# The last merge of a hybrid layer: low halves made by adding DMAs instead of GpSimd and VectorE subtractions

## The chip, the cores and the metric

The kernel runs on one core of a Trainium2 chip. The metric is the device time of one execution in microseconds. The engines are TensorE (PE, with its weight loads as PEld), VectorE (DVE), ScalarE (ACT), GpSimd (POOL) and SyncE (SP), which here only issues DMAs. Each engine works through its own queue in order. A DMA is issued by SP, or by POOL where it has to add to what stands at its destination; the data are then moved by 16 DMA engines that all queues share.

## The reference

One layer with two token groups, 128 context tokens and 512 latent tokens (640 in all), model width 1024:

```python
h = _rmsnorm(x, p["norm1_g"]) * (1.0 + sc1) + sh1
u_rw, u_na, gate_rw, gate_na = jnp.split(h @ p["w_in"], IN_SPLITS, axis=-1)
o_rw, s_new = _rwkv_branch(u_rw, s0, ...)
...
merged = (jax.nn.sigmoid(gate_rw) * (o_rw @ p["w_o_rwkv"])
          + jax.nn.sigmoid(gate_na) * (o_na @ p["w_o_na"]))
x = x + g1 * (merged @ p["w_out"])
h2 = _rmsnorm(x, p["norm2_g"]) * (1.0 + sc2) + sh2
x = x + g2 * ((jax.nn.silu(h2 @ p["ffn_w1"]) * (h2 @ p["ffn_w3"])) @ p["ffn_w2"])
```

o_rw and o_na have 512 features each, that is four blocks of 128. The change lies where `merged` is completed and multiplied by w_out.

## The kernel before, in words

All products are float32, computed in three passes: each operand is split into a high half (a cast to the fp32r type) and a low half (the value minus the cast high half), and TensorE adds high by high, high by low and low by high. So every weight tile of 128x1024 and every activation needs a cast (ScalarE, line 173 for weights, 185 and 1580 for activations) and a low half. For a weight tile `wcast` (166) makes the low half in one of two ways. With `eng` left out, VectorE subtracts (175). With `eng` = pool, ScalarE first writes the negated tile, rounded to fp32r, into the low tile (171), and POOL then issues a DMA that adds the staged weights to it (172). 37 weight tiles take this second way in the kernel before. For an activation `split` (184) casts and subtracts on a given engine (186).

The kernel runs through the projections, neighbourhood attention and the recurrent branch, the merge, w_out and the feed-forward part. The merge goes over eight output blocks of 128 features (index c8). Units "a" and "b" of `merge_gen` (1453) have already added up the products of seven of the eight feature blocks of o into `mt[c8]`. The eighth, the last output of the recurrent branch, is written by `out` (1388) for ct = 3 into two tiles `o3`, one high and one low, in two halves of 320 tokens; PRM["yo"] names for each ct the engine that makes the low half (1419).

Then comes the last merge, `last_gen` (1566). `wo` (1564) is the weight tile for the eighth feature block; `c0` (1589) is the first tile of w_out. For each c8 and each half (a, b) of 320 tokens, a group, `last_gen` issues three matmuls of wo by o3 (1576) into a PSUM tile, of which there are three, multiplies by the gate on VectorE (1577), adds `mt` on VectorE (1579), casts to the high half `mh` on ScalarE (1580) and makes the low half `ml` on POOL (1581). Tiles mh and ml hold the merged activation m; in the profile both are called m, and the gate tiles t are called pre (c8 under 4) and tr (the others).

`w_out_gen` (1585) multiplies m by w_out; it goes through `tok_gen` (261) with line 284. It takes the four weight tiles of the first half of the output columns in turn; with each it goes over two blocks of m, for the four latent token tiles and then the context tile, and for each of these three matmuls: mh by the weight's high half, ml by the high half, mh by the low half. The loop at 1593 weaves the two: PRM["lw"] is 0 for the first five groups and 2 for the other eleven, so after group 5 (counted from 0) and after each later one two matmuls of w_out are issued; the rest follows at the end (1597). 

In this block only TensorE's order is the written one (MANUAL, 78). Where VectorE, ScalarE, POOL and SP take up each instruction is set by a planner that simulates the program while it is built. In the recurrent part before and the second half of w_out behind it, TensorE, POOL, VectorE and ScalarE have a written order (FIRST, 79).

Weight tiles are staged by SP loads into `wst` buffers, two in the pool that wo and c0 use; the next tile that takes such a buffer can only be loaded when its last reader is done, be it an engine or a DMA. In the same stretch SP loads the five tiles of x (1548), the gate rows G (1553), the tiles t of the last four blocks (1570) and further tiles of w_out.

Of the kernel before, what the change touches and what calls it, by code (L numbers as in the profile page):

```python
# [7 lines left out]
F32 = mybir.dt.float32  # L8
F32R = mybir.dt.float32r
AF = mybir.ActivationFunctionType  # L10
ALU = mybir.AluOpType
# [58 lines left out]
    fp=(6, 12, 18), h2e="dpddddpddd", x0e="a", ze="aa", y2=1, y1=0, sc=3, sr=3, sp=1, mg=1.915, h1=0.952,  # L70
    h2=0.91, jobs=((2, 9, 28), (2, 9, 28), (2, 9, 28), (2, 11, 28)),
    mds=((4, 12), (4, 12), (4, 12), (4, 14)), bud=((1.8, 0.8), (1.3, 1.8)), off=6, tk=2, h3=1,
    h4=1.07, g1=2, km="dddddddd", kb="ddpd", ma="d", yo="pppp", r0="pd", rl=(0, 0, 0), lh=(0, 0, 1, 1),
    wl="dddddddddppppppppppppppppppppppppppdpppppppppppp", nu=9, jo=(2, 0, 1), na=(
        "6.0.12.0.1 6.0.12.0.0 6.0.12.0.0 6.0.12.0.2 6.0.12.0.0 6.0.12.0.2 6.0.12.0.0 6.0.12.0.2 6.0.12.0.0 "
        "6.0.12.0.2 6.0.12.1.0 6.1.12.1.2 6.2.12.2.0 6.1.12.2.2 6.0.12.2.0 6.1.12.1.2 6.2.14.2.0 "
# [25 lines left out]
def V(ap, dims, off=0):  # L102

    return bass.AP(ap.tensor, ap.offset + off, [list(ap.ap[0])] + [list(d) for d in dims])
# [3 lines left out]
def body(ctx: ExitStack, tc: tile.TileContext, xs, xp, cols, consts, w_ada, b_row, w_rw, w_qkv,  # L108
# [3 lines left out]
    pe, act, dve, pool, sp = nc.tensor, nc.scalar, nc.vector, nc.gpsimd, nc.sync  # L112

    def open_pool(stack, name, bufs=1, space=None):
        if space is None:
            return stack.enter_context(tc.tile_pool(name=name, bufs=bufs, reuse_waits="tile"))
        return stack.enter_context(tc.tile_pool(name=name, bufs=bufs, reuse_waits="tile", space=space))
# [17 lines left out]
    def nm(s):  # L135
        cn[0] += 1
        return f"{s}_{cn[0]}"
# [19 lines left out]
    def wdma(src, home=None):  # L157
        if len(rot) > 1 and home is None:
            rot.append(rot.pop(0))
        pl, nst, nhl = (rot if home is None else wpool)[-1 if home is None else home] if rot else wpool[-1]  # L160
        st = pl.tile([P, 1024], F32, tag="wst", bufs=nst, name=nm("wst"))
        n = src.shape[1] if len(src.shape) == 2 else 1024
        sp.dma_start(st[:, :n] if len(src.shape) == 2 else V(st[:, :], [[128, 8], [1, 128]]), src)
        return st, n, pl, nhl

    def wcast(w, eng=None):
        st, n, pl, nhl = w
        hi = pl.tile([P, 1024], F32R, tag="whi", bufs=nhl, name=nm("whi"))
        lo = pl.tile([P, 1024], F32R, tag="wlo", bufs=nhl, name=nm("wlo"))
        if eng is pool:  # L170
            act.activation(lo[:, :n], st[:, :n], AF.Copy, scale=-1.0)  # L171
            pool.dma_start(lo[:, :n].bitcast(F32), st[:, :n], accum_op=ALU.add)  # L172
        act.copy(hi[:, :n], st[:, :n])  # L173
        if eng is not pool:
            dve.tensor_tensor(out=lo[:, :n], in0=st[:, :n], in1=hi[:, :n].bitcast(F32), op=ALU.subtract)  # L175
        return hi, lo

    def wload(src, eng=None):
        return wcast(wdma(src), eng)
# [135 lines left out]
    def hilo(n):  # L315
        return [hp.tile([P, 8, NT], F32R, tag=f"hp{i}", bufs=1, name=f"{n}{i}") for i in range(2)]
# [141 lines left out]
    def pre_t():  # L458
        return kp.tile([P, 643], F32, tag="pre", bufs=4, name=nm("pre"))[:, :NT]
# [320 lines left out]
    with s1:  # L780
# [25 lines left out]
        with s1a:  # L806
            for b, dst, gcol in ((0, qT, dcol(dqg)), (1, kT, col("kg"))):
# [10 lines left out]
                for i in range(5):  # L818
# [10 lines left out]
                                      in0=V(qr[:, :], [[64, 8], [1, 64]]),  # L829
                                      in1=V(r[:, :], [[1, 8], [0, 64]]), op=ALU.mult)  # L830
                    if b == 1 and i == 4:
                        kout = tb.tile([P, 512], F32, tag="vt", bufs=2, name="kout")
                        dve.tensor_tensor(out=V(kout[:, :], [[64, 8], [1, 64]]),
                                          in0=V(qn[:, :], [[64, 8], [1, 64]]),
                                          in1=V(kgb[:, :], [[0, 8], [1, 64]]), op=ALU.mult)
# [4 lines left out]
                    for f in range(4):  # L840
                        src = pst[:, f * 128:(f + 1) * 128]
                        if i < 4:
                            out = V(dst[f], [[1, 2], [8, 64]], 2 * i)
                            src = V(src, [[64, 2], [1, 64]])
                        else:
                            out = dst[f][:, 512:640]
# [27 lines left out]
        with ExitStack() as s1b:  # L874
# [127 lines left out]
            with tc.manual_schedule(engines=FIRST):  # L1002
                for k, step in enumerate(PRM["na"].split()):
                    a, p, b, q, n = (int(x) for x in step.split("."))
# [556 lines left out]
    pp = open_pool(ctx, "pp4", bufs=3, space=PSUM)  # L1561

    mh, ml = hilo("m")
    wo = wload(w_o[:, :, 896:1024].rearrange("c p n -> p c n"))

    def last_gen():
        ts_ = []
        for c8 in range(8):
            t = pre_t() if c8 < 4 else trp.tile([P, NT], F32, tag="tr", bufs=4, name=nm("tr"))
            sp.dma_start(t, trw_d[c8])  # L1570
            ts_.append(t)
        for c8, t in enumerate(ts_):
            for (a, b) in halves:
                ps = pp.tile([P, 512], F32, tag="tp", name=nm("fl"))
                for n, (w, x) in enumerate(((wo[0], o3[0]), (wo[0], o3[1]), (wo[1], o3[0]))):
                    pe.matmul(ps[:, :H2], w[:, c8 * 128:c8 * 128 + 128], x[:, a:b], start=n == 0, stop=n == 2)
                dve.scalar_tensor_tensor(out=t[:, a:b], in0=t[:, a:b], scalar=1.0, in1=ps[:, :H2],
                                         op0=ALU.add, op1=ALU.mult)
                dve.tensor_tensor(out=t[:, a:b], in0=mt[c8][:, a:b], in1=t[:, a:b], op=ALU.add)
                act.copy(mh[:, c8, a:b], t[:, a:b])  # L1580
                pool.tensor_tensor(out=ml[:, c8, a:b], in0=t[:, a:b], in1=mh[:, c8, a:b].bitcast(F32),
                                   op=ALU.subtract)
                yield

    def w_out_gen(pss, ws, toks, **kw):
        return tok_gen(pss, pp, (mh, ml), ws, list(range(8)), toks, **kw)

    pss = {}
    c0 = wload(w_out[0])
    trp = open_pool(hs, "trp")  # L1590
    weights(hs, 2, 2)
    w0 = w_out_gen(pss, [c0] + [w_out[q] for q in range(1, 4)], range(5))
    with tc.manual_schedule(engines=MANUAL):
        for h, _ in enumerate(last_gen()):
            for _ in range(PRM["lw"][h]):
                next(w0)
        drain(w0)
# [378 lines left out]
def _build(arrays):  # L1976
    import concourse.bacc as _bacc

    nc = _bacc.Bacc("TRN2", target_bir_lowering=False, num_devices=1)
    args = [nc.dram_tensor(f"in_{n}_dram", v.shape, mybir.dt.from_np(v.dtype), kind="ExternalInput").ap()  # L1980
            for n, v in arrays.items()]
    args += [nc.dram_tensor(f"out_{i}_dram", s, F32, kind="ExternalOutput").ap()
             for i, s in enumerate(_OUTS)]
    with tile.TileContext(nc, **TCARGS) as tc:
        body(tc, *args)
    return nc
# [12 lines left out]
```

## Time and profile before

| | |
|---|---|
| median of 3 runs (lowest to highest) | 1192.29 us (1192.16 to 1193.37) |
| profiled execution, its time and its span | 1191.72 us, 1189.7 us |
| mean granted TensorE clock | 0.985 |
| TensorE busy | 1124.1 us (94%) |
| VectorE, ScalarE, POOL busy | 777.5, 530.5, 205.1 us |
| the last merge (first to last matmul of line 1576) | 679.0 to 695.3 us |
| first half of w_out complete | 720.77 us |

The last merge stands in the middle of the span. Times inside the span are counted from its first instruction. The page gives the busy time of every engine, the chain of work that ended last, and groups of instructions; the timeline gives the instructions of one engine in order, with the idle time before them and what ended it in brackets; stretches of the span can be asked for by engine, with the granted clock of TensorE (1.00 is full) and the busy share of the 16 DMA engines.

### The profile page before, as it was taken

Reading aid. Unit: us, or ns where it says so; the run is one execution under the profiler, and the core shown is the slowest. Engines: PE = TensorE matmul, PEld = TensorE weight load, DVE = VectorE, ACT = ScalarE, POOL = GpSimd, SP = SyncE. Lnnn points to the kernel's source line nnn. Section 1 sums busy time; section 2 is a strip of 40 time slices with the busy share of each in tenths; the row PEclk is TensorE's granted clock in tenths of the full one; section 3 lists DMA queues with packets and bytes.
Section 4 is the critical chain, followed back from the end, with each engine's and each line's share of the span. In section 5 each row is a group of like instructions: output and inputs, shape, how many; then the busy total and the mean of one; then the engine's idle time right before and its main releaser. Section 6 shows DMA issues by size and latency. Waiting matters only on the chain.

```text
span 1189.7 us, 26921 instructions
## 1 busy us (share of the span) xinstructions
PE 1124.1 (94%) x11160; PEld 998.3 (84%) x11160; DVE 777.5 (65%) x1630; ACT 530.5 (45%) x1053; POOL 205.1 (17%) x273
## 2 busy tenths in 40 slices
PE   6999999999999999999599799989999999999998
PEld 4688877789888988888488678889899989998997
DVE  4564455559469658836474675888568757775675
ACT  4444666554564664565133342654224422442340
POOL 1162244320111211111101250100001000000000
PEclk9999999999999999999799999999999999999999
DMA  9762767553333514433654851312312231232122
GB/s 335 265 117 84 244 216 230 191 146 98 103 93 84 153 50 104 123 93 79 200 138 110 245 218 54 107 49 79 104 57 86 89 107 54 89 100 90 59 75 103
DMA packets 61906, 149.42 MB, mean 126 GB/s; under 512 B 7732, under 2 KB 23732, under 8 KB 61784
## 3 DMA queue, kind: packets, MB, share of 16 engines
q1 hardware_dynamic: 55592, 131.56, 33.6%
q0 software_dynamic: 5328, 14.94, 6.8%
q8 instruction: 88, 1.44, 0.5%
q10 hardware_dynamic: 864, 1.20, 0.3%
q14 instruction: 34, 0.28, 0.1%
HBM read 118.41 MB, written 14.32 MB: 112 GB/s over the span
## 4 chain that ended last, share of the span: by engine, by line
PE 65%; DVE 8%; ACT 3%; DMA 2%; issue 1%; SPq 0%; ACTq 0%; DVEq 0%; POOLq 0%
PE f L1718 23%; PE acc L284 17%; PE fl L197 13%; DMA wlo<-wst 1%; DVE pr L1250 1%; PE w L1324 1%; PE w L1351 1%; DVE RL L1254 1%; PE mm L197 1%; PE w L1364 1%; PE w L1336 1%; PE w L1148 1%; DMA o<-o_d 1%; PE w L1196 1%; PE w L1126 1%
## 5 line engine op out<-in xcount | busy, mean ns | idle before, releaser
L1718 PE MATMUL f<-t,whi 128*128 128x320 f32 x640 | 141.4, 309 | 0.0
L1718 PE MATMUL f<-b,whi 128*128 128x320 f32 x608 | 136.5, 312 | 3.6 <-ACT b L185 1.8
L284 PE MATMUL acc<-whi,u 128*128 128x512 f32 (+1 forms) x448 | 136.0, 385 | 0.0
L197 PE MATMUL fl<-h,whi 128*128 128x320 f32 x704 | 126.5, 319 | 0.8 <-issue 0.8
L197 PEld LDWEIGHTS fl<-h,whi 128*128 128x128 f32 x704 | 106.1, 188 | 5.6 <-issue 0.9
L173 ACT CAST whi<-wst 128x1024 fp32r<-128x1024 f32 (+2 forms) x86 | 81.5, 953 | 64.7 <-PE acc L284 32.5
L1718 PEld LDWEIGHTS f<-t,whi 128*128 128x128 f32 x640 | 107.1, 188 | 0.0
L1718 PEld LDWEIGHTS f<-b,whi 128*128 128x128 f32 x608 | 103.0, 190 | 4.8 <-ACT b L185 2.2
L1718 PE MATMUL f<-t,wlo 128*128 128x320 f32 x320 | 98.9, 309 | 0.0
L284 PEld LDWEIGHTS acc<-whi,u 128*128 128x128 f32 x448 | 83.5, 188 | 16.7
L1718 PE MATMUL f<-b,wlo 128*128 128x320 f32 x304 | 94.7, 312 | 1.4 <-DVE wlo L1762 1.4
L1759 ACT CAST whi<-ws 128x1024 fp32r<-128x1024 f32 x40 | 42.0, 1051 | 108.7 <-PE f L1718 48.5
L1773 POOL TENSOR_TENSOR ws<-wst 128x512 f32<-128x512 f32 x20 | 28.2, 1409 | 341.3 <-DVE wlo L1762 226.7
L175 DVE TENSOR_TENSOR wlo<-wst,whi 128x1024 fp32r<-128x1024 f32 (+1 forms) x49 | 62.0, 1274 | 37.2 <-ACT whi L173 36.6
L284 PE MATMUL acc<-wlo,u 128*128 128x512 f32 (+1 forms) x224 | 86.3, 385 | 0.0
L284 PE MATMUL acc<-whi,h 128*128 128x512 f32 x240 | 78.0, 399 | 1.2 <-DVE h L398 1.1
L172 POOL DMA_DIRECT2D wlo<-wst x37 | 32.6, 881 | 232.4 <-ACT wlo L171 212.9
L1558 DVE SCALAR_TENSOR_TENSOR tt<-acc,G 128x512 f32<-128x512 f32 (+1 forms) x51 | 34.7, 681 | 50.5 <-PE acc L284 50.5
L197 PE MATMUL fl<-h,wlo 128*128 128x320 f32 x352 | 66.5, 321 | 0.0
L197 PE MATMUL fl<-o,whi 128*128 128x320 f32 x224 | 46.3, 337 | 16.8 <-DMA o<-o_d 10.0
L1759 ACT CAST whi<-wst 128x1024 fp32r<-128x1024 f32 (+1 forms) x48 | 41.3, 869 | 42.3 <-PE acc L284 37.6
L1718 PEld LDWEIGHTS f<-t,wlo 128*128 128x128 f32 x320 | 60.1, 188 | 0.0
(333 smaller groups left out, 2539.1 us busy)
## 6 DMA issues: line engine op xcount, KB each, us to landing
wst<-in_w_dram SPq DMA_DIRECT2D x66, 512.0 KB
wst<-in_w_rw_dram SPq DMA_DIRECT2D x31, 512.0 KB
wa<-in_w_ada_dram SPq DMA_DIRECT2D x24, 512.0 KB
wlo<-wst POOLq DMA_DIRECT2D x22, 512.0 KB, 4.5
f<-in_w_ada_dram SPq DMA_DIRECT2D x16, 512.0 KB
wst<-in_w_qkv_dram SPq DMA_DIRECT2D x12, 512.0 KB
o<-o_d SPq DMA_DIRECT2D x14, 320.0 KB
x<-in_xs_dram SPq DMA_DIRECT2D x8, 512.0 KB
```

Of the source, the lines that this page charges most:

```text
L172: pool.dma_start(lo[:, :n].bitcast(F32), st[:, :n], accum_op=ALU.add)
L173: act.copy(hi[:, :n], st[:, :n])
L175: dve.tensor_tensor(out=lo[:, :n], in0=st[:, :n], in1=hi[:, :n].bitcast(F32), op=ALU.subtract)
L197: pe.matmul(ps[:, :t1 - t0], w[:, a:a + 128], x[:, k0 + kt, t0:t1], start=n == 0, stop=n == 3 * nk - 1)
L284: pe.matmul(pss[i][:, a:b], lhs(x, kt, ts_), w[:, cs_], start=ki == 0 and n == 0, stop=ki == last and n == 2)
L1126: pe.matmul(t[r0:r0 + 32, 64 * i:64 * i + 64], S.BK[l // 10][own, l % 10, 0, 32 * bk:32 * bk + 32], V(AG[own, l, h, :], [[0, 2], [1, 32]], ...
L1148: pe.matmul(pr[h][hrows[h ^ i], o_], x[hrows[h], :], R_[hrows[h], l, :], start=True, stop=True)
L1196: pe.matmul(pt[h][hrows[h ^ i], o_], S.BK[l // 10][hrows[h], l % 10, i, :], idh(h), start=True, stop=True)
L1558: dve.scalar_tensor_tensor(out=tt, in0=ps[:, a:b], scalar=c, in1=G[:, g, sl], op0=ALU.mult, op1=ALU.mult)
L1718: pe.matmul(ps[:, :H2], w_[:, c_], x_[:, kt, :], start=first and kt + n == 0, stop=last and kt == 3 and n == 2, skip_group_check=more)
L1759: act.copy(r[0][:, :width], src())
L1773: eng_x(PRM["se"][i - 1]).tensor_tensor(out=o_, in0=x, in1=y, op=op)
```

## The change

The low half of `wo` and of `c0` is made with `eng` = pool: a negation on ScalarE, and a DMA issued by POOL that adds the staged weights. For c8 from 0 to 5, `ml` is made in the same manner: ScalarE negates each half of t into ml, and after the second half one DMA, issued by POOL, adds the whole t (128 x 640, 320 KB) to it. For c8 of 6 and 7, VectorE subtracts. The low half of the last output `o3` is made by VectorE instead of POOL. POOL has no tensor operation left in the last merge.

```diff
-    h4=1.07, g1=2, km="dddddddd", kb="ddpd", ma="d", yo="pppp", r0="pd", rl=(0, 0, 0), lh=(0, 0, 1, 1),
+    h4=1.07, g1=2, km="dddddddd", kb="ddpd", ma="d", yo="pppd", r0="pd", rl=(0, 0, 0), lh=(0, 0, 1, 1),
...
-    wo = wload(w_o[:, :, 896:1024].rearrange("c p n -> p c n"))
+    wo = wload(w_o[:, :, 896:1024].rearrange("c p n -> p c n"), pool)
...
                 act.copy(mh[:, c8, a:b], t[:, a:b])
-                pool.tensor_tensor(out=ml[:, c8, a:b], in0=t[:, a:b], in1=mh[:, c8, a:b].bitcast(F32),
-                                   op=ALU.subtract)
+                if c8 < 6:
+                    act.activation(ml[:, c8, a:b], t[:, a:b], AF.Copy, scale=-1.0)
+                    if a:
+                        pool.dma_start(ml[:, c8, :].bitcast(F32), t, accum_op=ALU.add)
+                else:
+                    dve.tensor_tensor(out=ml[:, c8, a:b], in0=t[:, a:b], in1=mh[:, c8, a:b].bitcast(F32),
+                                      op=ALU.subtract)
                 yield
...
-    c0 = wload(w_out[0])
+    c0 = wload(w_out[0], pool)
```

## The prediction

> **What bounds the kernel now.** I read the busy shares and the chain that ended last, then the chain in order of time around the last merge, then the timelines of the engines there.
>
> ```profile
> PE 1124.1 (94%) x11160; PEld 998.3 (84%) x11160; DVE 777.5 (65%) x1630; ACT 530.5 (45%) x1053; POOL 205.1 (17%) x273
> ...
> PE 65%; DVE 8%; ACT 3%; DMA 2%; issue 1%; SPq 0%; ACTq 0%; DVEq 0%; POOLq 0%
> ```
>
> ```profile
> 648.52 0.28 issue
> ...
> 675.80 1.24 DVE wlo L175
> ...
> 677.05 0.33 SPq L163
> ...
> 700.53 20.24 PE acc L284 x88
> ```
>
> TensorE is the bound. From 700.53 us on it runs without a break: 88 matmuls in 20.24 us are 0.23 us each, and the first half of w_out is complete at 720.77. The stretch after that is just as full:
>
> ```profile
> 676.00:679.00 3.00, 0.00 (x0) 0.00 (x1) 2.97 (x5) 0.60 (x3) 1.53 (x1) 1.00 0.31 74
> 679.00:684.00 5.00, 4.45 (x16) 3.82 (x17) 4.97 (x11) 1.62 (x3) 1.23 (x2) 0.58 1.00 400
> 679.85:686.65 6.80, 6.28 (x21) 5.68 (x21) 6.80 (x12) 1.37 (x4) 3.08 (x4) 0.50 1.00 405
> 684.00:692.00 8.00, 7.43 (x35) 6.46 (x34) 8.00 (x14) 2.78 (x7) 7.08 (x8) 0.84 1.03 415
> 701.00:1186.00 485.00, 479.79 (x2808) 444.31 (x2806) 340.54 (x477) 171.02 (x250) 36.91 (x30) 1.00 0.25 83
> ```
>
> (Columns: length, then busy time of PE, PEld, DVE, ACT, POOL, granted clock, DMA share, GB/s.) TensorE is busy 479.79 of 485 us, so what the end of the first w_out half gains or loses against 720.77 goes to the end of the kernel one for one. The whole question is the stretch from 676 to 701, where TensorE does not run full, the granted clock is 0.50 for 6.8 us, and the DMA engines are full (1.00 to 1.03).
>
> ```profile
> 675.34 0.60 PE L197 MATMUL fl<-o,wlo 128*128 128x320 f32 x3
> 679.03 0.53 PE L1576 MATMUL fl<-o,whi 128*128 128x320 f32 x2 [3.09 <-ACT o L185]
> ...
> 683.04 0.73 PE L1576 MATMUL fl<-o,whi 128*128 128x320 f32 x2
> ...
> 683.85 0.73 PE L1576 MATMUL fl<-o,whi 128*128 128x320 f32 x2
> ...
> 684.64 1.05 PE L284 MATMUL acc<-whi,m 128*128 128x512 f32 x2
> ...
> 692.26 0.46 PE L1576 MATMUL fl<-o,whi 128*128 128x320 f32 x2
> ...
> 692.71 0.40 PE L284 MATMUL acc<-wlo,m 128*128 128x512 f32 x1
> ...
> 700.53 0.50 PE L284 MATMUL acc<-wlo,m 128*128 128x512 f32 x1 [2.02 <-DVE wlo L175]
> ```
>
> The order on TensorE is written by hand: six groups of three L1576 matmuls (high by high, low by high, high by the weight's low), then two w_out matmuls, a group, two, and so on. The two at 684.64 are the first users of m: the first reads the high half of block 0, the second, at about 684.64+0.43 = 685.07, its low half. A group costs 0.45 us at full clock (692.26 to 692.71) and 0.81 at half (683.04 to 683.85).
>
> **The change part by part.** In these rows are the operations it touches:
>
> ```profile
> 674.72 1.05 ACT L173 CAST whi<-wst 128x1024 fp32r<-128x1024 f32 x1 [4.01 <-PE fl L197]
> ...
> 678.52 0.46 ACT L185 CAST o<-out 128x320 fp32r<-128x320 f32 x1 [2.40 <-DVE out L1412]
> ...
> 683.31 0.82 ACT L1580 CAST m<-pre 128x320 fp32r<-128x320 f32 x2 [3.38 <-PE fl L1576]
> ```
>
> ```profile
> 680.41 1.21 DVE L175 TENSOR_TENSOR wlo<-wst,whi 128x1024 fp32r<-128x1024 f32 x1
> 681.55 1.27 DVE L1577 SCALAR_TENSOR_TENSOR pre<-pre,fl 128x320 f32<-128x320 f32 x3
> ```
>
> ```profile
> L1579 DVE TENSOR_TENSOR pre<-mt,pre x8: 477/804/1209, 682.7 to 689.6; 128x320 f32<-128x320 f32 x8
> ```
>
> ```profile
> 676.21 1.53 POOL L186 TENSOR_TENSOR o<-out,o 128x320 fp32r<-128x320 f32 x1 [6.58 <-ACT o L185]
> 679.06 1.08 POOL L186 TENSOR_TENSOR o<-out,o 128x320 fp32r<-128x320 f32 x1 [1.32 <-ACT o L185]
> 683.85 2.78 POOL L1581 TENSOR_TENSOR m<-pre,m 128x320 fp32r<-128x320 f32 x3 [3.71 <-ACT m L1580]
> ```
>
> The kernel already makes 37 low halves by an adding DMA (L172). Their landing times are the prices of the change:
>
> ```profile
> DMA to landing us min/median/max: 2.9/4.5/8.5
> ```
>
> ```profile
> wlo<-wst POOLq DMA_DIRECT2D x1, 192.0 KB, 5.8
> ...
> wlo<-wst POOLq DMA_DIRECT2D x1, 256.0 KB, 8.5
> ...
> wlo<-wst POOLq DMA_DIRECT2D x1, 512.0 KB, 6.4
> ...
> wlo<-wst POOLq DMA_DIRECT2D x1, 512.0 KB, 4.4
> ```
>
> ```profile
> 664.39:669.39 5.00, 4.02 (x27) 3.52 (x27) 2.66 (x6) 1.66 (x4) 3.52 (x3) 1.00 1.01 276
> 565.23:570.23 5.00, 0.00 (x0) 0.00 (x0) 0.00 (x0) 0.21 (x1) 0.92 (x1) 0.69 0.97 311
> 259.69:264.69 5.00, 3.72 (x172) 3.27 (x172) 1.56 (x2) 2.71 (x4) 2.46 (x4) 1.00 1.01 223
> 296.42:301.42 5.00, 5.00 (x123) 4.57 (x124) 4.81 (x9) 2.76 (x6) 0.85 (x1) 1.00 0.62 138
> ```
>
> The four landings belong to the four stretches in the same order: under full DMA engines 5.8 us for 192 KB, 8.5 for 256 KB, 6.4 for 512 KB; with room (0.62), 4.4 for 512 KB.
>
> **wo's low tile.** Removed: one VectorE subtraction of 1.24 us that ended at 677.04, long before its first use (679.40). Added: a ScalarE negation as long as the cast, 1.05 us (674.72 to 675.77), 0.28 us to the issue (the 648.52 row), a DMA issue on POOL at 676.05, and a landing. Bounds 4.4 and 6.4 us; the DMA share is 0.31 up to 679 and 1.00 after, so I take 5.0, nearer the quiet row: 681.05. The third matmul of the first group waits for it, and with it everything on TensorE. The SP load that waited for the same staging buffer (677.05) now waits for the landing too, with the loads of x and of four merge tiles queued behind it on SP, or it is moved behind those; none of them has a reader on TensorE's path before 691, so nothing is charged.
>
> **The last output's low half on VectorE.** POOL's 1.53 and 1.08 us go, two VectorE operations of some 0.48 (the shortest L1579) come. The output is complete near 678 instead of 680.14. Worth nothing: the first group's third matmul waits for wo until 681.05.
>
> **c0's low tile.** The subtraction at 680.41 (1.21 us), which stood right in front of the first L1577, goes; the DMA that replaces it is queued on POOL ahead of m's first one and needs wo's route again. Its tile is first read after m's low half, so nothing is charged; the VectorE time it frees counts in the next step.
>
> **m's low halves.** Before, POOL made each half-block in about 0.93 us (2.78 for three) behind its cast, and TensorE had no wait for it. Now block 0 needs both halves: two casts and two negations on ScalarE, an issue, a landing. From wo's landing: the third matmul 0.47 at half clock; from the first L1577 to the end of both casts 2.58 us (681.55 to 683.31+0.82); 0.8 more, since the three L1577 that run first now wait for groups 1 and 2 at 0.81 each instead of finding them done; 0.41 for the last negation (half of 0.82); 0.28 to the issue. That is 4.54, so the issue is at 685.59. For 320 KB no row exists. Between 2.9 (the shortest of all) and 8.5, in a stretch whose share is 1.03, I take 6.0, between the 5.8 and the 6.4 of the full rows: landing at 691.59, where before the matmul ran at 685.07. During that wait TensorE has only what is left of the first six groups (681.05 + 0.47 + 5 x 0.81 = 685.6), VectorE and ScalarE run dry behind it, and POOL and SP have nothing that helps.
>
> What TensorE still has to do then is 119 w_out matmuls and 10 groups: 119 x 0.23 + 10 x 0.45 = 31.9 us. Blocks 1 to 5 land while it works on block 0's 12 matmuls and after; charged nothing. The subtractions of blocks 6 and 7 (four of 0.48 on VectorE) are covered, because VectorE's L1579 are no longer stretched: 0.48 instead of 0.80 in the median. The 2.02 us wait for VectorE's wlo at 700.53 goes for the same reason; next late there is the same tile's own cast and load, which I charge nothing. ScalarE's 14 new operations (12 x 0.46 + 2 x 1.05 = 7.6 us) fit into its idle time (1.37 busy of 6.8).
>
> **The clock.** A stall of some 6 us comes right before 691.59. Here 3.09 idle us were followed by 6.8 us at 0.50, and elsewhere a busy TensorE stood at half clock for 3.4 us:
>
> ```profile
> 345.30:348.70 3.40, 3.40 (x30) 3.08 (x29) 2.38 (x4) 2.23 (x6) 0.00 (x0) 0.50 0.78 154
> ```
>
> Half clock costs half its length of full work: 1.7 to 3.4 us; I take the middle, 2.5.
>
> **Sum.** 691.6 + 31.9 + 2.5 = 726.0 against 720.77: +5.2 us. The profiled execution took 1191.72 (span 1189.7), 0.57 under the median, so I add to the median: 1192.29 + 5.2 = 1197.5. Bounds of the unknown costs: high, wo 6.4, m 8.5, clock 3.4: 676.05+6.4+4.54+8.5+31.9+3.4 = 730.8, +10.0, 1202.3; low, wo 4.4, a chain without the 0.47 and the 0.8 (3.27), m 2.9, clock nothing: 676.05+4.4+3.27+2.9+31.9 = 718.5, -2.3, 1190.0.
>
> **The rule weighed.** Row first: 512 KB never landed in this trace under 4.4 us. The Trainium skill (DMA: Bandwidth & Descriptors, "Anatomy of one DMA") fits a POOL-issued DMA as 2.0 us plus bytes over 436 GB/s, an estimate of 3.2 us for 512 KB and 2.75 for 320 KB. By it the sum would be 676.05+3.2+4.54+2.75+31.9+2.5 = 720.9, no change; the trace disagrees by 1.2 us at least.
>
> **The rivals.** Each as a mechanism with its price.
> - The DMA engines leave the adds alone: both land with no other traffic in the way. The full share (1.03) speaks against it; that SP may hold its loads back behind wo's staging buffer speaks for it. wo 4.4 and m about 3.7 (between the 2.9 and the 4.4): 676.05+4.4+4.54+3.7 = 688.7, a stall of 3.7 us (from 680.45+0.47+4.05 = 685.0); if the clock holds, 688.7+31.9 = 720.6: 1192.1. By the rule above much the same comes out.
> - Faster: the freed VectorE outruns the adds. Without the subtraction at 680.41 and with unstretched L1579 the first block is ready early, and m's add takes the trace's shortest time: the low bound, 1190.0 and under. It decides from a landing before 686.5 on (686.5+31.9 = 718.4, 0.2% gained). For it speak POOL's share in the stretches above; against it that TensorE has nothing to do before wo lands.
> - Worse: the adds meet the burst of loads as at 565.23, where 256 KB took 8.5 us. Then 695.5 and the high bound, 1202.3. For it: the same share and the same mix of HBM loads; against it: one such landing in 37.
> - The change does not do what it says, that is VectorE's relief and the adds both stay off the path (wo's low tile lands before the last output is ready, m's before its use): it needs wo in under 3.4 us, which no 512 KB row shows.
>
> **How the numbers follow.** Forecast (a stall, then half clock, 1195 to 1200) 0.50; the burst 0.16; the quiet DMAs with the clock held 0.15, and the page's fit 0.03, both without change; the faster case 0.14, of which 0.11 beyond the bound; no moved limit 0.02, without change. 0.2% (2.4 us) is about what a measurement of this kernel can tell from none. Slower 0.66, same 0.23, faster 0.11. The range reaches from the low bound to the high one, 1190.0 to 1202.3; the forecast's own is 1195 to 1200.
>
> **What would show it.** Right: TensorE waits at L1576 for a DMA of wlo near 681 and at the second L284 for a DMA of m for 4 to 7 us; a granted clock of 0.50 behind that; L1579 near 0.48; no 2.02 us at the next wlo; the first w_out half ends near 726. Wrong: m's add lands within 4 us of its issue, the planner finds an order that has wo's add issued earlier, the clock stays at 1.00, or TensorE's later stretch is not full and swallows the shift.

## The result and the profile after

| | before | after |
|---|---|---|
| median (lowest to highest) | 1192.43 us (1192.16 to 1193.37) | 1208.08 us (1205.78 to 1209.56) |
| ratio, 95% interval | | 1.0127 [1.0112, 1.0142] |
| profiled execution, its span | 1191.72, 1189.7 us | 1209.56, 1207.7 us |
| first half of w_out complete | 720.77 us | 738.92 us |

The change costs 15.6 us, three times the forecast of 5.2. The kernel after is the slower one on the whole interval, and above the forecast's range (1202.3).

The profiled execution of after is 1.5 us over its median, that of before 0.7 under. Of the difference between the two, 2.1 us are older than the first instruction that the change touches: an adding DMA that both kernels have, ahead of the last merge, starts 1.47 us later and takes 0.63 longer, and the load of wo waits for it (issued at 670.21 in before, at 672.30 in after). The chain of before, and then the chain of after:

```profile
664.39 5.76 DMA wlo<-wst
```

```profile
665.86 6.39 DMA wlo<-wst
```

This 2.1 us is called the shift below. So 18.15 us between the two ends of the first w_out half, less 2.1, are 16.1 us that the changed stretch adds in this execution. Behind it TensorE is as full as before (460.03 busy of 465.10 us), so what is lost here is lost for good. TensorE's timeline shows where:

```profile
680.15 1.66 PE L197 MATMUL fl<-o,whi 128*128 128x320 f32 x6 [1.84 <-DVE mx L1464]
682.59 0.87 PE L1576 MATMUL fl<-o,whi 128*128 128x320 f32 x2
683.26 0.47 PE L1576 MATMUL fl<-o,wlo 128*128 128x320 f32 x1
...
686.25 0.40 PE L284 MATMUL acc<-whi,m 128*128 128x512 f32 x1
697.44 0.77 PE L284 MATMUL acc<-whi,m 128*128 128x512 f32 x1 [10.79 <-DMA m<-pre]
...
709.34 0.90 PE L1576 MATMUL fl<-o,whi 128*128 128x320 f32 x2 [5.28 <-DVE tr L1577]
```

Three waits are to be read here: 1.84 us for VectorE ahead of the merge, 10.79 us for m's first add, and 5.28 us for VectorE in the middle of it. The third matmul of the first group, on wo's low tile (683.26), waits for nothing. The stretches between (length, then PE, PEld, DVE, ACT, POOL, granted clock, DMA share, GB/s) show what TensorE could do:

```profile
686.65:697.44 10.79, 0.00 (x2) 0.03 (x1) 2.20 (x6) 3.34 (x9) 2.58 (x3) 0.69 1.02 277
697.44:701.00 3.56, 3.56 (x11) 3.19 (x12) 1.28 (x3) 0.00 (x0) 0.00 (x0) 0.50 1.08 275
...
706.00:709.34 3.34, 0.00 (x0) 0.00 (x1) 2.08 (x4) 3.13 (x6) 0.00 (x0) 0.78 1.03 422
709.34:714.30 4.96, 4.96 (x14) 4.05 (x15) 4.45 (x10) 3.10 (x10) 1.58 (x2) 0.50 0.80 243
714.30:738.90 24.60, 24.60 (x111) 20.22 (x109) 12.12 (x21) 6.06 (x10) 0.99 (x2) 0.99 0.27 70
738.90:1204.00 465.10, 460.03 (x2721) 428.20 (x2720) 329.35 (x466) 167.40 (x246) 33.82 (x27) 1.00 0.24 83
```

The two long stalls are each followed by work at half clock: 3.56 and 4.96 us, which cost half their length, 4.3 us. From 697.44 to 738.92 there are 41.5 us: 31.9 of work, as forecast, 5.28 of the later wait and 4.3 of half clock.

The first add was issued at 687.21 (685.59 forecast, and 2.1 for the shift makes 687.7) and landed 10.1 us later, where 6.0 was taken. The bracket in its line names a load of x; ScalarE's last negation of block 0 ended at 686.93, the forecast's 0.28 us before the issue. The second and third add took 10.9 and 12.0 us. GpSimd's timeline, then the landings by issue, of the first of m's adds and of the fourth, issued when the burst of loads was about to end (the two behind it took 3.6 and 3.8 us):

```profile
687.21 0.86 POOL L1584 DMA_DIRECT2D m<-pre  x1 [2.16 <-DMA x<-in_xs_dram]
...
710.05 0.86 POOL L1584 DMA_DIRECT2D m<-pre  x1 [18.54 <-ACT m L1582]
```

```profile
m<-pre POOLq DMA_DIRECT2D x1, 320.0 KB, 10.1
...
m<-pre POOLq DMA_DIRECT2D x1, 320.0 KB, 3.9
```

The second stall begins, in part, on SyncE. The loads in the same stretch, before and then after:

```profile
677.05 0.33 SPq L163 DMA_DIRECT2D wst<-in_w_out_dram  x1
677.44 2.04 SPq L1548 DMA_DIRECT2D x<-in_xs_dram  x4
...
683.93 1.62 SPq L163 DMA_DIRECT2D wst<-in_w_out_dram  x2
```

```profile
675.26 7.71 SPq L163 DMA_DIRECT2D wst<-in_w_out_dram  x2
683.03 1.98 SPq L1548 DMA_DIRECT2D x<-in_xs_dram  x4
...
690.47 3.83 SPq L163 DMA_DIRECT2D wst<-in_w_out_dram  x2
```

The second load of the group at 675.26 takes the staging buffer of wo, which is free only when wo's add, issued at 678.18, has landed at 682.6:

```profile
wlo<-wst POOLq DMA_DIRECT2D x1, 512.0 KB, 4.4
```

Behind it on SyncE everything is late: the loads of x by 5.6 us (677.44 to 683.03) and with them w_out[1] by 6.5 (683.93 to 690.47), 2.1 us of each the shift. ScalarE's timeline, then VectorE's, then the chain (whose load of 693.96 is the second of the group at 690.47) show what that does:

```profile
706.18 1.04 ACT L173 CAST whi<-wst 128x1024 fp32r<-128x1024 f32 x1 [15.83 <-DMA wst<-in_w_out_dram]
707.13 0.45 ACT L1580 CAST m<-pre 128x320 fp32r<-128x320 f32 x1
```

```profile
707.26 1.22 DVE L175 TENSOR_TENSOR wlo<-wst,whi 128x1024 fp32r<-128x1024 f32 x1 [6.08 <-ACT whi L173]
708.40 0.48 DVE L1579 TENSOR_TENSOR pre<-mt,pre 128x320 f32<-128x320 f32 x1
```

```profile
683.97 9.98 DMA x<-in_xs_dram
...
693.96 13.45 DMA wst<-in_w_out_dram
```

The cast of w_out[1] stands in ScalarE's queue ahead of the cast of m's block 3, its subtraction in VectorE's ahead of block 3's L1579, and the tile they wait for lands at about 706. TensorE stands still for 5.28 us over a tile that it doesn't need yet.

Last, the DMA engines themselves. The queues of before from 674 to 705 us (packets, MB, share of the 16 engines' time), and of after from 689.2 to 702, while adds are moving (the line of GB/s has 40 equal slices of that stretch):

```profile
q1 hardware_dynamic: 2596, 8.46, 71.4%
```

```profile
GB/s 243 294 282 294 256 294 269 269 282 282 218 282 256 317 280 320 278 320 250 325 224 338 291 317 282 304 278 296 309 229 256 301 264 264 264 296 272 224 264 376
...
q0 software_dynamic: 575, 1.51, 60.8%
q1 hardware_dynamic: 662, 2.10, 45.1%
```

q0 is POOL's queue. 60.8% of 12.8 us for 1.51 MB are 5.2 us of all engines per MB added; a load costs 2.75 here and 2.6 in before (71.4% of 31 us for 8.46 MB). While adds and loads are mixed, all engines are busy and move some 280 GB/s, against 400 to 415 in the full stretches of before. So the adds also slow the loads that they meet.

### The profile page after: what moved, and what is told of

Read it like the earlier page. It is cut to its first block, busy times and chain, and to the rows that moved or that the text cites. A ratio compares the mean times of both kernels' runs of the same rounds, so it can differ in the third digit from the quotient of the medians.

```text
span 1207.7 us, 26940 instructions
## 1 busy us (share of the span) xinstructions
PE 1127.8 (93%) x11160; PEld 1000.8 (83%) x11160; DVE 769.9 (64%) x1634; ACT 536.5 (44%) x1067; POOL 191.5 (16%) x263
## 4 chain that ended last, share of the span: by engine, by line
PE 61%; DVE 9%; DMA 4%; ACT 3%; issue 2%; SPq 0%; DVEq 0%; ACTq 0%
PE f L1723 21%; PE acc L284 17%; PE fl L197 11%; DMA wst<-in_w_out_dram 1%; DMA wlo<-wst 1%; DVE pr L1250 1%; PE w L1351 1%; PE w L1324 1%; PE w L1364 1%; DMA x<-in_xs_dram 1%; DVE RL L1254 1%; PE mm L197 1%; PE w L1336 1%; DMA o<-o_d 1%; PE w L1148 1%
## 5 line engine op out<-in xcount | busy, mean ns | idle before, releaser
L284 PE MATMUL acc<-whi,u 128*128 128x512 f32 (+1 forms) x448 | 136.0, 385 | 0.0
L197 PE MATMUL fl<-h,whi 128*128 128x320 f32 x704 | 126.5, 319 | 0.5 <-issue 0.5
L197 PEld LDWEIGHTS fl<-h,whi 128*128 128x128 f32 x704 | 106.1, 188 | 5.3 <-issue 0.6
L284 PEld LDWEIGHTS acc<-whi,u 128*128 128x128 f32 x448 | 83.5, 188 | 16.7
L175 DVE TENSOR_TENSOR wlo<-wst,whi 128x1024 fp32r<-128x1024 f32 (+1 forms) x47 | 57.6, 1233 | 45.5 <-ACT whi L173 44.9
L284 PE MATMUL acc<-wlo,u 128*128 128x512 f32 (+1 forms) x224 | 86.3, 385 | 0.0
L284 PE MATMUL acc<-whi,h 128*128 128x512 f32 x240 | 78.0, 399 | 1.0 <-DVE h L398 1.0
L197 PE MATMUL fl<-h,wlo 128*128 128x320 f32 x352 | 66.6, 321 | 0.0
L197 PE MATMUL fl<-o,whi 128*128 128x320 f32 x224 | 47.9, 344 | 18.6 <-DMA o<-o_d 10.0
L284 PE MATMUL acc<-whi,m 128*128 128x512 f32 x160 | 52.4, 403 | 10.8 <-DMA m<-pre 10.8
```

The source lines that it names most:

```text
L197: pe.matmul(ps[:, :t1 - t0], w[:, a:a + 128], x[:, k0 + kt, t0:t1], start=n == 0, stop=n == 3 * nk - 1)
L284: pe.matmul(pss[i][:, a:b], lhs(x, kt, ts_), w[:, cs_], start=ki == 0 and n == 0, stop=ki == last and n == 2)
```

## The experiments

Losses are differences of medians to the kernel before on the same chip. "Issue" and "landing" are those of m's first add in the profiled execution. Each landing is thus of one execution, and they scatter: the add of 192 KB ahead of the merge that all these kernels share (at 664.39 in before) took 5.2 to 7.4 us in their profiles.

| run | what it is | loss, us | ratio, 95% interval | issue | landing |
|---|---|---|---|---|---|
| after | the change | +15.6 | 1.0127 [1.0112, 1.0142] | 687.21 | 10.1 |
| e1_m_only | m's part alone | +9.5 | 1.0085 [1.0062, 1.0108] | 686.62 | 8.2 |
| e2_tiles_only | wo and c0 alone | +2.7 | 1.0023 [1.0010, 1.0035] | | |
| e3_yo_only | last output on VectorE alone | +1.0 | 1.0011 [1.0002, 1.0021] | | |
| e4_wo_back | the change without wo's add | +11.1 | 1.0092 [1.0066, 1.0118] | 686.04 | 8.9 |
| e5_x_late | x loads moved in the source | +8.3 | 1.0077 [1.0052, 1.0101] | 685.10 | 8.9 |
| e7_m_on_vector | m on VectorE, the rest changed | +3.4 | 1.0027 [1.0015, 1.0039] | | |
| e9_x_gated | x held | +8.9 | 1.0078 [1.0063, 1.0093] | 686.17 | 10.3 |
| e12_before_x_gated | before, x held | +0.3 | 1.0001 [0.9987, 1.0014] | | |
| e15_x_G_gated | x and G held | +8.7 | 1.0072 [1.0044, 1.0100] | 686.03 | 10.8 |
| e16_m_only_x_G_gated | m's part alone, x and G held | +1.7 | 1.0016 [1.0003, 1.0029] | 683.36 | 5.0 |
| e17_m_vector_only | before, m on VectorE | -2.1 | 0.9983 [0.9971, 0.9995] | | |
| e18_one_add | e1 with the add for block 0 alone | +8.5 | 1.0074 [1.0047, 1.0102] | 688.11 | 8.1 |
| e19_gated_c0_back | as e15, c0 on VectorE | +7.8 | 1.0069 [1.0044, 1.0094] | 687.21 | 8.5 |
| e20_gated_wo_back | as e15, wo on VectorE | +3.9 | 1.0034 [1.0022, 1.0046] | 688.38 | 6.8 |

### Which part carries the loss

e1_m_only puts only the change of `ml` into before; e2_tiles_only only the two `pool` arguments:

```diff
-    wo = wload(w_o[:, :, 896:1024].rearrange("c p n -> p c n"))
+    wo = wload(w_o[:, :, 896:1024].rearrange("c p n -> p c n"), pool)
...
-    c0 = wload(w_out[0])
+    c0 = wload(w_out[0], pool)
```

> Only the six adds of m (and VectorE for blocks 6 and 7); both weight tiles and the last output as before. Collision theory (the add of wo holds SP, so the loads of x, tr and w_out start 5 us later, onto the adds of m; w_out's second tile then comes late and holds ScalarE): without wo's add SP is not held past 677 us; the first add of m still meets the second half of the burst, lands in 6 to 9 us, TensorE waits 4 to 7 us there, and no second wait over 2 us follows: +5 to +9 us. Landing theory (the wait for m's first landing and the clock behind it are the whole price, whatever SP does): +13 us or more, since nothing of m's part is changed.

> Only wo and c0 by adds; m's low halves and the last output on POOL as before. Collision theory: the planner puts the loads of x ahead of the w_out load that waits for wo's buffer, so SP is not held; wo's add now meets the loads of x, lands in 5 to 8 us and is waited for by TensorE: +1 to +4 us. Landing theory: wo is not on the path, within 1 us of before.

m's part alone costs 9.5 us, with a wait of 9.16 us for the add at L284. The landing (8.2 us) is as the collision theory had it, but the wait and the loss are above its 4 to 7 and 5 to 9 us, and a second wait is there though SyncE isn't held:

```profile
703.32 0.56 PE L1576 MATMUL fl<-o,whi 128*128 128x320 f32 x2 [2.65 <-DVE pre L1577]
```

The two tiles cost 2.7 us as a median over ten executions that lie between 1193.3 and 1199.5, a spread no wider than that of before on the same chip (1188.5 to 1194.8). The profiled one is the longest of these, so how much TensorE waits in the others isn't known. In it SyncE issued x ahead of the load that waits for wo's buffer, wo's add landed only after 10.6 us, and TensorE waited for it:

```profile
689.24 0.64 PE L1576 MATMUL fl<-o,wlo 128*128 128x320 f32 x1 [7.99 <-DMA wlo<-wst]
```

e3_yo_only has the third part alone:

```diff
-    h4=1.07, g1=2, km="dddddddd", kb="ddpd", ma="d", yo="pppp", r0="pd", rl=(0, 0, 0), lh=(0, 0, 1, 1),
+    h4=1.07, g1=2, km="dddddddd", kb="ddpd", ma="d", yo="pppd", r0="pd", rl=(0, 0, 0), lh=(0, 0, 1, 1),
```

> Before with only the last output's low half moved from GpSimd to VectorE. In the three runs that have that move, the last three L197 matmuls wait for VectorE's mx (L1464) for 1.84, 3.79 and 2.71 us, and in the two runs without it they don't. If this move is a part of the loss, +1.5 to +3.5 us and that wait is there; if the move is free, as the prediction had it, the time stays within 1 us of before.

About 1 us, between the two expectations and at the lower edge of what a measurement can tell. Its trace shows the wait: VectorE now makes the last output's low half, behind wo's subtraction, and the merge step that TensorE needs (L1464) stands behind that. VectorE's timeline, then TensorE's:

```profile
675.57 1.22 DVE L175 TENSOR_TENSOR wlo<-wst,whi 128x1024 fp32r<-128x1024 f32 x1 [2.65 <-ACT whi L173]
676.72 0.48 DVE L186 TENSOR_TENSOR o<-out,o 128x320 fp32r<-128x320 f32 x1
677.12 0.48 DVE L1464 SCALAR_TENSOR_TENSOR mx<-mx,fl 128x320 f32<-128x320 f32 x1
```

```profile
677.65 1.51 PE L197 MATMUL fl<-o,whi 128*128 128x320 f32 x6 [3.40 <-DVE mx L1464]
```

The three parts add up to 13.2 of 15.6 us. The rest only comes when they are together, and e4 shows where from.

e4_wo_back is the change with wo's low tile left on VectorE (the first pair of lines above, the other way round):

> The changed kernel with wo's low tile on VectorE again. Collision theory: SP goes on at about 677 us as before, the burst starts 5 us earlier, m's first add lands in 6 to 8 us instead of 10.1, and ScalarE is not held for w_out's second tile: +5 to +9 us over before. Landing theory: unchanged, +13 to +17 us, as wo's add was never waited for by TensorE.

4.5 of the 15.6 us go: the second stall shrinks from 5.28 to 2.69 and 0.78 us, since SyncE isn't held behind wo's buffer. It doesn't go altogether here, nor in e1 (2.65 us): the hold makes up a part of it, and the rest comes with m's adds. That the rest is the loads of w_out, slowed by the adds, fits the queues above but wasn't isolated. m's first add still takes 8.9 us to land, so +11.1 lies between the two expectations; by its interval the loss is 7.9 to 14.1 us.

e7_m_on_vector leaves out only m's adds from the change (`ml` is a `dve.tensor_tensor` subtraction for all eight blocks):

> The changed kernel with all low halves of m as subtractions on VectorE: no add of m, no negation of m. If m's adds carry the loss, the 10.8 us wait at L284 is gone and +3 to +6 us stay (the two tiles' adds 2.7, the last output 2 to 3). If VectorE's load is the reason why adds looked better than subtractions (sixteen more operations of 0.48 to 0.8 us on VectorE), TensorE waits for VectorE at L284 and L1576 instead and +9 or more stay.

+3.4, as the theory of m's adds had it. SyncE is held behind wo's buffer here as in after (w_out[1] is issued at 690.63), and yet the second stall is gone with m's adds: by these runs the hold makes it longer but doesn't make it alone. The next late thing is c0's low tile, whose add is in the same burst:

```profile
694.57 0.80 PE L284 MATMUL acc<-wlo,m 128*128 128x512 f32 x1 [5.55 <-DMA wlo<-wst]
```

### What makes the landing long

e5_x_late moves the loads of x in the source from line 1547 to behind the block. SyncE still issued them at 683.71, ahead of m's first add (685.10), so it doesn't hold them back from it.

> The changed kernel with the five loads of x issued behind the first half of w_out's tiles instead of ahead of them. Collision theory: 2.5 MB leave the burst, m's first add lands in 5 to 7 us, w_out's second tile is there in time, the second wait (5.3 us at L1576) goes: +4 to +8 us over before. Landing theory: the first wait stays at 9 us or more: +12 to +16 us.

The landing fell only to 8.9 us, above the expected 5 to 7, and the loss to +8.3, largely because the tiles of w_out now came ahead of x and the second stall of 5.28 us went (1.62 us are left). To hold the loads back in earnest, e9_x_gated takes them out at 1547 as well and gives them something to wait for:

```diff
+    for i in range(5):
+        pool.tensor_copy(x2[i][:, 0:1], ml[:, 0, 319:320].bitcast(F32))
+        sp.dma_start(x2[i], xs[i * 128:(i + 1) * 128, :] if i < 4 else xp)
     hs.close()
```

> The changed kernel with the five loads of x (2.5 MB) made to wait until m's first add has landed: each x tile first gets one column of m's low block 0 by a GpSimd copy, which its load overwrites. If the loads of x are what m's first add meets, its landing falls from 10.1 us to 5 to 7, the wait at L284 from 10.8 to 5 to 8 us and the loss from 15.6 to +8 to +12. If the landing is long whatever else moves (the adds of one queue behind each other, or the tile's shape), it stays at 9 to 11 us and the loss at +13 to +17.

The loads of x now start at 696.85, and the landing is still 10.3 us: a miss for the theory that x is what the add meets. The loss falls to 8.9 us all the same, because the second stall is gone: behind the wait for the add (10.53 us) TensorE has none left in the merge. The control, before with the same gate, shows that the late x costs nothing and brings nothing:

> Before with the same late loads of x, as the control. If the gate itself and the later x cost nothing, within 1 us of before. If the burst of loads also hurts the kernel before (stretched L1579, the wait of 3.09 us, half clock), 1 to 4 us faster. If x now comes too late for its reader behind the first half of w_out, 1 us or more slower.

e15_x_G_gated holds G too, by a copy of the same column into each row of G ahead of its load; e16_m_only_x_G_gated does that to m's part alone:

> The changed kernel with the loads of x and of G (3.5 MB) held until m's first add has landed. With x alone held, the add still took 10.3 us, with 2 MB of other loads issued in the four us before it. If the landing is set by the bytes of loads that are queued when the add is issued, 1 MB less at the 280 GB/s of that stretch makes it 10.3 to about 6.5 us and the loss +5 to +8. If it is set by the adds themselves (c0's in front, at 5.3 us of all engines per MB), it stays at 9 to 10.5 us.

> Only m's part of the change, with the loads of x and of G held until the first add has landed: no add in front of it, and the fewest loads that the kernel can do with (tr and two or three tiles of w_out). By queued loads: landing 4.5 to 6.5 us (8.2 with the loads), loss +3 to +6 against +9.5. By a price of the add itself: 8 us again and +8 to +10.

e15 falsifies the simple sum over the held loads: 10.8 us, with 3.5 MB out of the way. e16 has the same m adds and the same held loads, and there the first one lands in 5.0 us and the whole loss is 1.7 us, less than the 3 to 6 expected. So a long landing is no property of m's adds. e18_one_add is the other end: one single add for block 0, all loads as in before, and blocks 1 to 7 subtracted on VectorE. Its edit, here against e1:

```diff
-                if c8 < 6:
+                if c8 < 1:
```

> Before with one single add: block 0 of m by a DMA that adds, blocks 1 to 7 on VectorE, everything else and all loads as in before. If the loads make the landing long, it is 7 to 9 us here too (8.2 with two more adds behind it), the wait at L284 6 us or more and the loss +5 to +9. If it is the number of adds, the one alone lands in 4 to 6 us and the loss is +1 to +4.

One add alone lands after 8.1 us and costs 8.5, nearly as much as six (9.5 in e1). It isn't the number of adds. (e17 below differs from e18 in block 0 alone, which VectorE subtracts there too; the one add makes 10.7 us between their medians.) How it spends its time is in the queues. e18 from the issue (688.11) to 692.61, and from there to the end of the wait (696.33):

```profile
q1 hardware_dynamic: 579, 1.57, 99.0%
```

```profile
q1 hardware_dynamic: 303, 0.86, 61.1%
q0 software_dynamic: 144, 0.33, 46.3%
```

For 4.5 us after its issue not one packet of the add moves, while loads fill the engines; then its 0.33 MB (144 packets) pass within 3.7 us. In e16 the same lag is 2.0 us (683.36 to 685.36, with 102.9% loads), and from then on the adds have the engines nearly to themselves:

```profile
q0 software_dynamic: 240, 0.57, 97.5%
q1 hardware_dynamic: 56, 0.16, 13.1%
```

In after itself c0's add, issued at 684.19, moves nothing until 689.19 (95.8% loads). wo's add, issued at 678.18 into nearly idle engines (5% in the next 0.8 us), has its first packet 1.4 us later. The add of 710.05 does too, though loads fill 91% of the first 1.5 us: they are the last of the burst. Once adds move they aren't starved: in after, 575 of their packets pass beside 662 of loads. The Trainium skill (DMA: Bandwidth & Descriptors, "Queues, rings and completion order") has each engine take turns between the queues that have work, a packet at a time; the near-equal counts agree with that, and the lag before the first packet isn't explained by it. Nor does the lag follow VectorE's work: VectorE is as busy beside the add of 710.05 (4.45 of 4.96 us) as beside c0's (2.92 of 3.00 us from 684), and in e18 it is idle for the last 1.5 us of the lag.

What remained was why e15 has 10.8 us and e16 5.0. Two things differ that touch the DMA engines: c0's add stands in front of m's, and wo's add holds SyncE, so that the four loads of tr (1.3 MB) are issued at 681.77, four us ahead of m's add, and not at 675.63, eight us ahead of it. e19 takes away the one, e20 the other:

> The changed kernel with x and G held, and w_out[0]'s low tile back on VectorE, so that no add stands in front of m's first. If c0's add (0.5 MB at 5.3 us of all engines per MB, 2.8 us) is what kept the landing at 10.8 us with x and G held, it falls to 7.5 us or less and the loss from 8.7 to +4 to +6. If the loads of tr, which wo's add still holds back on SyncE, are the reason, it stays at 9 us or more and the loss at +7 or more.

> The changed kernel with x and G held, and wo's low tile back on VectorE, so that SyncE isn't held behind wo's staging buffer and issues the four loads of tr (1.3 MB) some 4 us earlier against m's add; c0's add stays in front. If the held loads are the reason, the landing falls from 10.8 to 7.5 us or less and the loss to +4 to +6; if c0's add is, it stays at 9 us or more and the loss at +7 or more.

The landings of e15, e19 and e20, as the list of issues gives them:

```profile
m<-pre POOLq DMA_DIRECT2D x1, 320.0 KB, 10.8
```

```profile
m<-pre POOLq DMA_DIRECT2D x1, 320.0 KB, 8.5
```

```profile
m<-pre POOLq DMA_DIRECT2D x1, 320.0 KB, 6.8
```

By these profiles c0's add accounts for 2.3 us of the landing, wo's hold on SyncE for 4.0; the two together, 6.3, are about the 5.8 between e15 and e16. 2.3 us is no more than the scatter of one add between executions, so c0's part is weakly shown. And the bytes of loads don't order the landings: e19, with x and G (3.5 MB) held, takes 8.5 us, e18, with all loads there, 8.1. In time only the second counts: e19 is at +7.8, as slow as e15 within its interval, because VectorE's subtraction for c0, back in its place, has m's add issued later (687.21 instead of 686.03; 17.3 instead of 15.6 us behind the issue of wo's load). e20 is at +3.9 with the landing that was expected of the held loads; e19's landing lies between its two expectations.

### m's low halves on VectorE

e17_m_vector_only is before with one line changed, `dve.tensor_tensor` for `pool.tensor_tensor` at 1581:

> Before with one thing changed: m's low halves are made by VectorE instead of GpSimd, without an add. If VectorE is the engine that holds this stretch (it is busy 27.5 of 29 us there), sixteen more operations of 0.48 us make it 2 to 6 us slower; if GpSimd's operations beside it cost VectorE as much (its L1579 take 0.80 instead of 0.48), the time stays within 1 us, or is a little shorter.

It is the one version below both kernels: 1190.62 us, 2.1 under before, 0.17% with an interval of 0.05 to 0.29%, so just clear of the spread. The rows are those of line 1579, and the stretch from 676 to 701, of e17 (which runs about 1 us later here than before did); that of before follows:

```profile
L1579 DVE TENSOR_TENSOR pre<-mt,pre x8: 477/484/490, 684.0 to 691.6; 128x320 f32<-128x320 f32 x8
```

```profile
676.00:701.00 25.00, 20.38 (x88) 17.28 (x87) 23.39 (x50) 11.37 (x20) 2.61 (x2) 0.80 0.77 300
```

```profile
676.00:701.00 25.00, 18.86 (x82) 15.69 (x83) 24.93 (x41) 10.77 (x21) 16.93 (x16) 0.86 0.73 285
```

VectorE does nine more operations in the stretch and is busy 1.5 us less. Its L1579 take 0.484 us instead of 0.804 in the median when GpSimd doesn't work beside it. The Trainium skill (SBUF — State Buffer, "Who interferes with whom") says that a VectorE operation with two inputs in SBUF contends with a GpSimd one that reads SBUF; the trace agrees. That VectorE could be relieved by taking GpSimd's work away from beside it, rather than by adding DMAs, is what the prediction saw only half.

## Why the prediction was wrong

The direction was right, and the mechanism (a wait for m's add, then half clock) was there; the size was three times too small. Step by step, on the profiled execution and without its 2.1 us of shift:

- **wo's add, 5.0 us, as what the first group waits for.** The third matmul of the first group came at 683.26 - 2.1 = 681.2, which is the forecast moment (681.05), by another cause: the add took 4.4 us and was hidden, and the last output was late (1.84 us for VectorE's L1464 at the last L197, with ScalarE's negation ahead of its cast). The number was right by luck, the reason wrong.
- **The last output's low half on VectorE, worth nothing.** Wrong by about 1 us (e3): the step looked at when the output is ready and not at what stands behind it in VectorE's queue.
- **c0's add, nothing charged.** The net was right beside m's adds (e15 and e19 differ by less than their intervals), with some 2.3 us more of landing and 1.7 less to the issue. Without m's adds its landing is itself waited for (5.55 us in e7); m's wait hid it.
- **m's chain to the issue, 4.54 us.** About right: the issue came at 687.21 - 2.1 = 685.1, 0.5 us ahead of the forecast 685.59.
- **The landing, 6.0 us.** The term that was mis-sized most: 10.1. The rows of 5.8, 6.4 and 8.5 us under full engines were averaged as if full were full. The runs show that it goes by what is in the queues when the add is issued, though not in proportion to the bytes: 3.6 to 3.9 us once the burst was over or about to end, 5.0 behind tr that is nearly through (e16), 8.1 and 8.2 behind all loads (e18, e1), 8.9 with c0's add in front as well (e4), and 8.9 to 10.8 with SyncE held by wo's too (e5, after, e9, e15). The row of 8.5, which the rival of the burst took, was near for an add alone. The fit of the Trainium skill (DMA: Bandwidth & Descriptors, "Anatomy of one DMA") that the prediction weighed, an estimate of 2.75 us, wasn't reached by any of them (3.6 at the least).
- **The SyncE loads held behind wo's buffer, nothing charged; no second wait.** The step that failed outright. Beside the shift they moved by 3.5 to 4.4 us; they were pushed into m's add (4.0 us of landing in e15 against e20), and w_out[1] came so late that its cast blocked ScalarE's and VectorE's queues and stalled TensorE for 5.28 us, of which some 2.7 to 3.5 us are there without the hold too (e1, e4), and nothing with the hold but without m's adds (e7). The prediction asked who on TensorE reads these tiles, and not who stands behind their casts.
- **The clock, 2.5 us.** Half of 3.56 and of 4.96 us, 4.3: right for the first stall, and once more for the second, which wasn't foreseen. The remaining work of 31.9 us was right.

The forecast of +5.2 and these misses, 4.1 for the landing, 5.28 for the second stall and 1.8 for the clock, less the 0.5 of the issue, make 15.9 of the 16.1 us. L1579 near 0.48 us came as forecast (0.485 in the median), and the 2.02 us wait at the next wlo did go, but its VectorE work was late all the same. Of the rivals the burst was the nearest, with 8.5 us and 1202.3, and it still held the second stall at nothing.

## What to carry to other kernels

The landing of an adding DMA goes by the loads that are open when it is issued: here 3.6 to 10.8 us for the same 320 KB, and not by a simple sum of bytes. So an add belongs where a transfer that late hurts nobody, or ahead of the burst, and not on the path in the middle of it. Where an add is the last reader of a staging buffer, ask which loads wait for that buffer in the issuing queue, where they will land instead, and what casts stand in front of useful work until they do. Before work is taken off an engine by DMAs, look at whether its operations are only stretched by another engine beside it: moving sixteen subtractions onto the busy VectorE was 2.1 us faster than before, and the change, which hands twelve of them to DMAs, was 15.6 us slower.

## What was unexpected of the hardware

- An add issued in the middle of the burst of loads moved no packet for 4.5 us (e18) and 5 us (c0's add in after), against 2.0 us in e16 and 1.4 us for wo's add into nearly idle engines. Why it is so long isn't shown by any run.
- A MB of adds took 5.2 us of all DMA engines, a MB of loads 2.75 beside them; engines that were fully busy moved some 280 GB/s with adds among the loads, against 400 to 415 with loads alone.
- One and the same add, 192 KB ahead of the merge, took 5.2 to 7.4 us in the profiles of sixteen kernels that have it in common.

What stays open: 2.4 of the 15.6 us that the three parts alone don't add up to are put down to wo's hold on SyncE by e4 and e20, but weren't isolated; how much of the second stall the hold makes and how much the slower loads, was not separated; and the lag before an add's first packet was seen and not explained.
